# A gradient along rows: the first store held back behind a matmul, and the last but one tile computed and stored in two rows

## The chip, the cores and the metric

The kernel runs on one core of a Trainium2 chip. The metric is the device time of one execution in microseconds (us); the profile's span, which covers the program's own instructions, is 1.8 to 2.6 us shorter.

## The reference, cut to what matters

```python
def setup_inputs():
    return {"x": np.random.randn(8192, 8192).astype(np.float32)}

def reference(x):
    return np.gradient(x, axis=1)
```

Inside a row the result is half the difference of the two neighbours; at both ends it is the plain difference. 268 MB are read and 268 MB written, and there is almost no arithmetic.

## The kernel before

The matrix is cut into 32 tiles of 128 partitions by two rows of 8192 floats (8.39 MB). Three slots hold them. A tile is loaded to column 64 of its slot, the vector engine writes half the differences from column 0, and the store reads from there. All loads and stores are issued by one engine (SyncE) into one queue, in the order three loads, three stores, three loads, and so on.

```python
    with tc.manual_schedule():
        for i in range(NB):                      # NB = 3
            load(i)
        for i in range(nsets):                   # nsets = 32
            ...
            ins = nc.gpsimd.tensor_sub(out=ends[:, i, :, :], ...)   # both edges, waits for the load
            at = [chain(i, ins, loads[i])]
            last = i == nsets - 1
            nr = 1 if last else R                # R = 2 rows; the last tile goes row by row
            for r in range(0, R, nr):
                ...
                ins = nc.vector._custom_dve(dve_ops.TENSOR_TENSOR_REDUCE_SUB_MAX, out=b[:, c0:c1],
                    in0=b[:, SH + c0 + 1 : SH + c1 + 1], in1=b[:, SH + c0 - 1 : SH + c1 - 1], ...)
                halved = chain(i, ins, *at)
                placer = nc.gpsimd if i % 5 in (1, 3) and not last else nc.vector
                ins = placer.tensor_copy(out=res[:, :, 0 : m : m - 1], in_=ends[:, i, r : r + nr, :])
                placed = chain(i, ins, halved)
                ins = nc.sync.dma_start(out=out_sets[i, :, ...], in_=b[:, ...])
                stores[i] = chain(i, ins, placed)
                at = [halved]
            if i % NB == NB - 1:
                for k in range(i + 1, min(i + 1 + NB, nsets)):
                    load(k)                      # waits for the store of the same slot
```

The edge copy (`tensor_copy`) puts the two end columns into the result; of every five tiles two have it done by GpSimd, the others by the vector engine.

## Time and profile before

| | before |
|---|---|
| median at first, 3 runs | 1247.24 us (1247.1 to 1248.14) |
| span of the profiled run | 1245.0 us |
| vector engine busy | 45% |
| DMA, mean over the span | 431 GB/s |

The DMA engines bound the kernel; the prediction shows the lines. A "turn" below is the point where the queue passes from loads to stores or back: near 62, 178, 294 us from loads to stores, near 120 and 236 back to loads. In the windows of the DMA, the share of a 1 us stretch in which exactly sixteen 64 KB packets start (1049 GB/s), one on each engine, is at once their mean duration in us. The usual one is 2.42. In the kernel before, the last packets ahead of the turns near 120, 178 and 236 (the turn near 62, at 3.37, stands in the prediction; columns: stretch, its length, vector engine, GpSimd, clock, DMA share, GB/s):

```profile
116.90:117.90 1.00, 0.00 (x0) 0.00 (x0) 1.00 2.42 1049
174.80:175.80 1.00, 1.00 (x1) 0.00 (x0) 1.00 2.42 1049
232.90:233.90 1.00, 0.00 (x0) 0.00 (x0) 1.00 2.42 1049
```

These three turns cost nothing; of the first four, only the one near 62 did.

### The profile page before, as it was taken

Reading aid. Unit: us, or ns where it says so; the run is one execution under the profiler, and the core shown is the slowest. Engines: PE = TensorE matmul, PEld = TensorE weight load, DVE = VectorE, ACT = ScalarE, POOL = GpSimd, SP = SyncE. Lnnn points to the kernel's source line nnn. Section 1 sums busy time; section 2 is a strip of 40 time slices with the busy share of each in tenths; the row PEclk is TensorE's granted clock in tenths of the full one; section 3 lists DMA queues with packets and bytes.
Section 4 is the critical chain, followed back from the end, with each engine's and each line's share of the span. In section 5 each row is a group of like instructions: output and inputs, shape, how many; then the busy total and the mean of one; then the engine's idle time right before and its main releaser. Section 6 shows DMA issues by size and latency. Waiting matters only on the chain.

```text
span 1245.0 us, 241 instructions
## 1 busy us (share of the span) xinstructions
DVE 554.8 (45%) x54; POOL 8.8 (1%) x48
## 2 busy tenths in 40 slices
DVE  2850483079009603850582079009603840591083
POOL 0000000000000000000000000000000000000000
DMA  9999999999999999999999999999999999999999
GB/s 404 438 436 419 425 438 438 438 438 438 434 427 421 436 438 438 436 438 432 432 419 438 436 438 432 436 434 432 423 436 436 436 438 436 430 427 430 436 411 404
DMA packets 9361, 536.88 MB, mean 431 GB/s; under 512 B 1040, under 2 KB 1040, under 8 KB 1040
## 3 DMA queue, kind: packets, MB, share of 16 engines
q1 hardware_dynamic: 9360, 536.88, 99.8%
q14 instruction: 1, 0.01, 0.0%
HBM read 268.44 MB, written 268.44 MB: 431 GB/s over the span
## 4 chain that ended last, share of the span: by engine, by line
another core or an unknown queue 74%; DVE 18%; DMA 3%; issue 2%; POOL 1%; SPq 0%; POOLq 0%
DVE slot L81 18%; DMA slot<-in_x_dram 3%; POOL ends L70 0%; POOL slot L92 0%; SPq L60 0%; DVE slot L92 0%; POOLq L127 0%
## 5 line engine op out<-in xcount | busy, mean ns | idle before, releaser
L81 DVE CUSTOM_DVE_ANT_0 slot<-slot 128x16382 f32<-128x16382 f32 (+1 forms) x33 | 551.3, 16706 | 667.9 <-POOL ends L70 667.9
L70 POOL TENSOR_TENSOR ends<-slot 128x4 f32<-128x4 f32 x32 | 6.3, 198 | 988.8 <-DMA slot<-in_x_dram 988.8
L92 DVE COPY slot<-ends 128x4 f32<-128x4 f32 (+1 forms) x21 | 3.6, 172 | 0.7
L92 POOL COPY slot<-ends 128x4 f32<-128x4 f32 x12 | 2.3, 190 | 207.9 <-DVE slot L81 207.9
L116 POOL MEMSET const-bfloat16-1.0<- 128x1 bf16 x1 | 0.1, 102 | 0.0
L116 POOL MEMSET const-uint8-127<- 128x1 uint8 x1 | 0.1, 102 | 0.0
L116 POOL MEMSET const-float32-0.0<- 128x1 f32 x1 | 0.1, 99 | 0.2 <-issue 0.2
L116 POOL MEMSET const-float32-1.0<- 128x1 f32 x1 | 0.1, 99 | 0.0
## 6 DMA issues: line engine op xcount, KB each, us to landing
out_dram<-slot SPq DMA_DIRECT2D x2, 4096.0 KB, 20.2
slot<-in_x_dram SPq DMA_DIRECT2D x32, 58.0
out_dram<-slot SPq DMA_DIRECT2D x31, 40.3
```

Source lines behind the costliest of these rows:

```text
L70: ins = nc.gpsimd.tensor_sub(out=ends[:, i, :, :], in0=xin[:, :, 1 : m : m - 2], in1=xin[:, :, 0 : m - 1 : m - 2],)
L81: ins = nc.vector._custom_dve(dve_ops.TENSOR_TENSOR_REDUCE_SUB_MAX, out=b[:, c0:c1], in0=b[:, SH + c0 + 1 : SH + c1 + 1], in1=b[:, SH + c0 ...
L92: ins = placer.tensor_copy(out=res[:, :, 0 : m : m - 1], in_=ends[:, i, r : r + nr, :])
L116: nc = _bacc.Bacc("TRN2", target_bir_lowering=False, num_devices=1)
```

## The change

It has two intents. The first store, which stood in the queue from 40 us on, is to come after the third load is through, so that it finds every engine idle. And tile 30, the last but one, is to be stored in halves so that its first half is in the queue before the last load ends.

```diff
+    psum = ctx.enter_context(tc.tile_pool(name="psum", bufs=1, space=bass.MemoryType.PSUM))
+    unread = psum.tile([1, 128], f32, name="unread", tag="unread")
...
+    def follow(ins, needed, reason):
+        edge = mybir.DependencyInfo(mybir.DependencyClass.Sync, mybir.DependencyReason.DATA)
+        tc.add_manual_dep(ins.ins, needed.ins.name, edge, reason=reason)
...
-            last = i == nsets - 1
+            last = i >= nsets - 2
...
-                placer = nc.gpsimd if i % 5 in (1, 3) and not last else nc.vector
+                placer = nc.gpsimd if i % 5 in (1, 3) and not last or i == nsets - 2 else nc.vector
...
+                if i == 0:
+                    at = [halved]
+                    first = placed
+                    continue
+                if i == 1:
+                    pause = nc.tensor.matmul(
+                        out=unread[:], lhsT=slots[0][:, 0:1], rhs=slots[0][:, 0:128], start=True, stop=True
+                    )
+                    follow(pause, placed, "towards the end of the third load")
+                    follow(store(0, 0, R, first), pause, "after the third load")
+                store(i, r, nr, placed)
```

The matmul's result is never read; it is a delay.

More of the change, by code (lines that the diff above doesn't have):

```diff
@@ L4 @@
 import concourse.tile as tile
-from concourse import bass_utils, dve_ops
+from concourse import bass_utils, dve_ops, mybir
 from concourse._compat import with_exitstack
@@ L61, in load, with store @@
         loads.append(chain(i, ins, *([stores[i - NB]] if i >= NB else [])))
+    def store(i, r, nr, *needed):
+        ins = nc.sync.dma_start(
+            out=out_sets[i, :, r * m : (r + nr) * m], in_=slots[i % NB][:, r * m : (r + nr) * m]
+        )
+        stores[i] = chain(i, ins, *needed)
+        return ins
     with tc.manual_schedule():
@@ L90 @@
                 res = b[:, r * m : (r + nr) * m].rearrange("p (t m) -> p t m", m=m)
-                placer = nc.gpsimd if i % 5 in (1, 3) and not last else nc.vector
+                placer = nc.gpsimd if i % 5 in (1, 3) and not last or i == nsets - 2 else nc.vector
                 ins = placer.tensor_copy(out=res[:, :, 0 : m : m - 1], in_=ends[:, i, r : r + nr, :])
                 placed = chain(i, ins, halved)
-                ins = nc.sync.dma_start(
-                    out=out_sets[i, :, r * m : (r + nr) * m], in_=b[:, r * m : (r + nr) * m]
-                )
-                stores[i] = chain(i, ins, placed)
+                if i == 0:
[5 more added lines that the diff above has]
+                        out=unread[:], lhsT=slots[0][:, 0:1], rhs=slots[0][:, 0:128], start=True, stop=True
+                    )
+                    follow(pause, placed, "towards the end of the third load")
+                    follow(store(0, 0, R, first), pause, "after the third load")
+                store(i, r, nr, placed)
                 at = [halved]
```

## The prediction

> **What bounds the kernel now.** I read the page first, then the waits, then the order in time at both ends, then the DMA windows in 1 us steps. The page (busy time of the engines, then the DMA part):
>
> ```profile
> span 1245.0 us, 241 instructions
> ...
> DVE 554.8 (45%) x54; POOL 8.8 (1%) x48
> ...
> DMA  9999999999999999999999999999999999999999
> ...
> HBM read 268.44 MB, written 268.44 MB: 431 GB/s over the span
> ```
>
> No compute engine is busy for half of the span and the 16 DMA engines are full in every slice, so the kernel ends when 536.88 MB have passed through them. The unit is one load or store of 8.39 MB. In order of time, GpSimd's first small operation on a tile starts when that tile's load has landed, so its start times are landing times. Here are the first two groups of three loads (first column start in us, second duration):
>
> ```profile
> 22.70 0.20 POOL L70 TENSOR_TENSOR ends<-slot 128x4 f32<-128x4 f32 x1 [22.26 <-DMA slot<-in_x_dram]
> ...
> 42.04 0.20 POOL L70 TENSOR_TENSOR ends<-slot 128x4 f32<-128x4 f32 x1 [19.14 <-DMA slot<-in_x_dram]
> ...
> 59.56 0.19 POOL L92 COPY slot<-ends 128x4 f32<-128x4 f32 x1 [17.32 <-DVE slot L81]
> 62.45 0.20 POOL L70 TENSOR_TENSOR ends<-slot 128x4 f32<-128x4 f32 x1 [2.71 <-DMA slot<-in_x_dram]
> ...
> 139.84 0.20 POOL L70 TENSOR_TENSOR ends<-slot 128x4 f32<-128x4 f32 x1 [77.19 <-DMA slot<-in_x_dram]
> ...
> 159.18 0.20 POOL L70 TENSOR_TENSOR ends<-slot 128x4 f32<-128x4 f32 x1 [1.64 <-DMA slot<-in_x_dram]
> ...
> 178.54 0.20 POOL L70 TENSOR_TENSOR ends<-slot 128x4 f32<-128x4 f32 x1 [19.16 <-DMA slot<-in_x_dram]
> ```
>
> From the second to the third landing takes 20.41 us in the first group and 19.36 in the second; first to second is 19.34 in both. Six transfers lie between the landings at 139.84 and 255.87 (the next group), 116.03 us, so one transfer takes **19.34 us** (434 GB/s). 64 of them are 1237.7 us. The other 7.3 us of the span are: the first landing 3.4 us later than one transfer, 1.07 us in the third load, 0.9 us of closing steps after the last store (whose wait ends at 1244.14), and about 2.0 us in the later groups: the landings at 62.45 and 1205.53 are 59 transfers apart, 1143.08 us against 1141.06. The later third loads took 19.36, 19.36, 19.39, 19.85, 19.96, 20.01, 19.52, 19.62 and 19.35, so the loss sits at the turn from loads to stores, and not in every group.
>
> The DMA windows (last column GB/s, by when a packet starts; 1049 is sixteen packets of 64 KB, one per engine) show both places that the change touches:
>
> ```profile
> 58.00:59.00 1.00, 1.00 (x1) 0.00 (x0) 1.00 3.37 1049
> 59.00:60.00 1.00, 0.49 (x1) 0.19 (x1) 1.00 0.00 0
> 60.00:61.00 1.00, 0.00 (x0) 0.00 (x0) 1.00 0.00 0
> 61.00:62.00 1.00, 0.00 (x0) 0.00 (x0) 1.00 2.28 983
> ```
>
> ```profile
> 1202.00:1203.00 1.00, 1.00 (x1) 0.00 (x0) 1.00 0.61 262
> 1203.00:1204.00 1.00, 0.81 (x2) 0.00 (x0) 1.00 0.00 0
> 1204.00:1205.00 1.00, 0.00 (x0) 0.00 (x0) 1.00 2.30 983
> 1205.00:1206.00 1.00, 0.24 (x1) 0.20 (x1) 1.00 0.15 66
> ```
>
> The third load's last sixteen packets start in 58 to 59 us and the first store's in 61 to 62: the share 3.37 says that these took 3.37 us each where 2.42 is usual. At the tail only four packets start in 1202 to 1203, none in the next us, and all sixteen engines start again after 1204: twelve engines stood idle for 1 to 2 us, because the store of tile 30 was issued at 1203.88, when four late engines were just finishing their last load.
>
> **What the Trainium skill says.** "DMA: Bandwidth & Descriptors", Where 436 GB/s comes from, gives a ceiling of 435 GB/s; the trace's 434 agrees, so nothing is to be had from the rate. The same page, Queues, rings and completion order, says that each engine consumes descriptors in ring order; the trace agrees, as the store issued at 40.39 moves nothing until the third load is through, over 20 us later. Its Latency and other measured facts puts the first byte of such an issue at about 0.6 us; here it is longer: the issue at 1203.88 starts packets after 1204.5 (in half-us windows, 1966 GB/s in 1204.5 to 1205.0), some 0.9 us, and the first load at 0.74 starts packets in 1.5 to 2.0. "TensorE: Matmul & The Clock Gate", Single matmul latency, gives (219 + N)/1.2 ns for a lone cold bf16 matmul, 0.29 us at N = 128; this one is float32, for which I estimate 0.3 to 0.9 us. The kernel before has no matmul, so no trace here shows it.
>
> **The change part by part.**
> *First store.* It is no longer issued at 40.39 but after a matmul that waits for tile 1's edge copy (59.56 + 0.19 = 59.75). With 0.6 us for the matmul the issue comes at about 60.4 to 60.7, and the first packets 0.9 us on, at **61.3 to 61.6**. The third load has no store behind it. I take its last packets to need the usual 2.42 us, ending at 60.6 to 61.2, with a landing at 42.04 + 19.34 = 61.4 instead of 62.45. So the 1.07 us of slow packets are exchanged for 0.3 to 1.0 us of idle engines: the first store starts 0 to 0.5 us earlier than before, I take **0.3**. The second store is issued directly behind it, far ahead of its turn, so no later wait moves.
> *Later turns.* All engines begin the first store together. In the tail of the kernel before, an idle start put 15 of 16 first packets in the same half us. If the 2.0 us of later loss come of engines that have drifted apart (four were about 2 us late at the end), a common start might shrink it; the trace does not show the cause, and the second group lost nothing without any such start. I count half: **1.0 us**, the least certain term.
> *Tile 30 in two rows.* One vector instruction of 17.23 us becomes two of about 8.69 (tile 31 already runs so), and GpSimd's two copies of 0.19 lie beside them. The first half's store is issued near 1186.42 + 8.7 + 0.3 = 1195.4, some 8 us before the ring runs dry, so the idle stretch of the twelve engines goes. But the end is set by the four late engines, which had none: from the last landing (1205.53) to the end of the last store's wait is 38.61 us, two transfers at 19.34 being 38.68. The tail loses nothing on the path, so this part is worth **0** while the same engines are late, up to a few tenths otherwise. The vector engine is free at 1203.8, before tile 31 lands; its two halves and stores stay hidden behind the store of tile 30.
> Sum: 0.3 + 1.0 + 0 = 1.3 us off a span of 1245.0. The median of 1247.24 is 2.2 above the span, and I keep that: 1247.24 - 1.3 = 1245.9.
>
> **The rivals.** (a) The matmul, the only one of the program, on an engine that has done nothing for 60 us, takes 1.5 to 3 us with its waits, and the idle gap outgrows the slow packets: 1248 to 1250. For it: no row to read its cost from. Against it: a semaphore releases GpSimd's copy within 0.1 us in this trace. (b) The load-to-store loss comes of the turn from reading to writing, not of drift, and engines in step all pay it at once, 1 us at each of ten turns as in the first group: some 1255. Against it: the engines were within half a us of each other at the second turn, which cost nothing. (c) All drift goes: 2.0 + 0.3 off, 1244.9. (d) The tail's gap is worth its full 2 us: against it stand the 38.61 us.
>
> **Range and chances.** Removing all loss after the start (1.07 + 2.0 us) without any idle gap ends at 1244.2, the low edge. The high edge is the slow matmul of (a) at its milder end with no gain elsewhere, 1248.0; the three runs before also spread over 1.0 us. For 2% the time would have to move by 25 us, far more than any rival gives: within 2% at 0.98.
>
> **What would show it.** A matmul of under 1 us from about 59.8, and the store's issue after it near 60.6; in the windows, last load packets of the usual length, then an empty us, then sixteen packets together near 61.5; the third landing near 61.4. The later third-load distances tell whether the drift shrank: all at 19.34 to 19.4 is rival (c), all at 20.4 is (b). At the tail a store issue near 1195, no empty us, and again 38.6 us from the last landing to the end. The prediction is wrong if the first store's packets start after 62, or if the late turns lose much more than 2 us.

## The result, and the profile after

| | before | after |
|---|---|---|
| median, 4 runs each | 1247.42 us (1247.1 to 1248.14) | 1249.51 us (1248.56 to 1249.63) |
| ratio | | 1.0014, 95% interval 0.9997 to 1.0032 |
| span of the profiled run | 1245.0 us | 1247.1 us |

A ratio is the mean time of one kernel's fast runs over that of the other's fast runs of the same rounds, so it is not quite the ratio of the medians. The class "within 2%" was right. The time was not: 1245.9 was predicted, and 1249.51 lies above the range's high end of 1248.0. By these runs alone the interval still just reaches 1.0; every kernel with the late store in the experiments lay on the same side.

In order of time (start, duration), the profile after shows the matmul, the issue behind it, the early landings and the end:

```profile
41.91 0.20 POOL L84 TENSOR_TENSOR ends<-slot 128x4 f32<-128x4 f32 x1 [19.12 <-DMA slot<-in_x_dram]
...
59.67 0.59 PE L116 MATMUL unread<-slot 128*1 128x128 f32 x2 [59.67 <-POOL slot L106]
60.29 18.98 SPq L71 DMA_DIRECT2D out_dram<-slot  x3
61.25 0.20 POOL L84 TENSOR_TENSOR ends<-slot 128x4 f32<-128x4 f32 x1 [1.63 <-DMA slot<-in_x_dram]
...
140.23 0.20 POOL L84 TENSOR_TENSOR ends<-slot 128x4 f32<-128x4 f32 x1 [78.78 <-DMA slot<-in_x_dram]
...
159.58 0.20 POOL L84 TENSOR_TENSOR ends<-slot 128x4 f32<-128x4 f32 x1 [1.64 <-DMA slot<-in_x_dram]
...
179.93 0.20 POOL L84 TENSOR_TENSOR ends<-slot 128x4 f32<-128x4 f32 x1 [20.15 <-DMA slot<-in_x_dram]
...
1188.33 17.42 DVE L95 CUSTOM_DVE_ANT_0 slot<-slot 128x8190 f32<-128x8190 f32 x2 [59.85 <-POOL ends L84]
1197.08 8.91 POOL L106 COPY slot<-ends 128x2 f32<-128x2 f32 x2 [8.79 <-DVE slot L95]
1205.82 19.88 SPq L71 DMA_DIRECT2D out_dram<-slot  x4
```

The third load lands 19.34 us after the second (61.25 less 41.91), where it was 20.41 before: its slow packets are gone. But the landing at 179.93 comes 20.35 us after the one at 159.58, where it was 19.36: the loss has come back one group later. And at the end GpSimd's two copies take 8.91 us, of which the second takes its usual 0.19, so that the first store of tile 30 goes out at 1205.82 and not near 1195.

The DMA windows of the kernel after (here with columns for TensorE and its weight loads ahead of the vector engine): last packets before the turns near 61, 120, 178 and 236, then the stretch around the first store.

```profile
57.80:58.80 1.00, 0.00 (x0) 0.00 (x0) 1.00 (x1) 0.00 (x0) 1.00 2.42 1049
116.80:117.80 1.00, 0.00 (x0) 0.00 (x0) 0.00 (x0) 0.00 (x0) 1.00 3.18 1049
175.30:176.30 1.00, 0.00 (x0) 0.00 (x0) 1.00 (x1) 0.00 (x0) 1.00 3.43 1049
234.30:235.30 1.00, 0.00 (x0) 0.00 (x0) 0.00 (x0) 0.00 (x0) 1.00 2.42 1049
...
60.00:61.00 1.00, 0.26 (x2) 0.00 (x0) 0.00 (x0) 0.00 (x0) 1.00 0.01 0
61.00:62.00 1.00, 0.00 (x0) 0.00 (x0) 0.51 (x1) 0.20 (x1) 1.00 2.47 1049
```

Near 61 the packets are now of the usual length (2.42). In exchange the turn near 120, free before, costs 3.18 - 2.42 = 0.76 us, and the turn near 178, free before, costs 1.01. The turn near 236 is free again.

Landings, and the issue of the fourth load, which waits for the first store to land, tell where the time went:

| event | before | after | after less before |
|---|---|---|---|
| third load lands | 62.45 | 61.25 | -1.20 |
| first store landed, fourth load issued | 81.78 | 81.14 | -0.64 |
| fourth load lands (turn near 120 passed) | 139.84 | 140.23 | +0.39 |
| seventh load lands (turn near 178 passed) | 255.87 | 257.20 | +1.33 |
| tile 30 lands | 1186.19 | 1188.09 | +1.90 |
| span | 1245.0 | 1247.1 | +2.1 |

### The profile page after: what moved, and what is told of

It reads as the page before. It is cut to its first block, busy times and chain, and to the rows that moved or that the text cites. A ratio compares the mean times of both kernels' runs of the same rounds, so it can differ in the third digit from the quotient of the medians.

```text
span 1247.1 us, 250 instructions
## 1 busy us (share of the span) xinstructions
PE 0.6 (0%) x2; PEld 0.1 (0%) x2; DVE 554.8 (44%) x54; POOL 17.8 (1%) x50
## 4 chain that ended last, share of the span: by engine, by line
another core or an unknown queue 74%; DVE 19%; DMA 3%; POOL 1%; issue 0%; SPq 0%; POOLq 0%
DVE slot L95 19%; DMA slot<-in_x_dram 3%; POOL slot L106 1%; POOL ends L84 0%; SPq L67 0%; DVE slot L106 0%; POOLq L151 0%
## 5 line engine op out<-in xcount | busy, mean ns | idle before, releaser
L106 POOL COPY slot<-ends 128x4 f32<-128x4 f32 (+1 forms) x14 | 11.2, 800 | 216.7 <-DVE slot L95 216.6
```

## The experiments

Twelve kernels ran. Of one call, all ran on the same chip beside runs of the kernel before.

### The parts one by one

Four of the twelve (`rows_only_gpsimd`, `rows_only_vector`, `late_third_store`, `late_fourth_load`) are made from the kernel before, and `before_again` is that kernel. `both_vector` is made from the change, and the other six from the change with tile 30 whole as before.

Theories: the 2 us come of the two turns (turn theory), or of GpSimd's slow copy at the end (copy theory). `late_store_only` is the change with tile 30 whole as before:

```diff
-            last = i >= nsets - 2
+            last = i == nsets - 1
-   placer = nc.gpsimd if i % 5 in (1, 3) and not last or i == nsets - 2 else nc.vector
+   placer = nc.gpsimd if i % 5 in (1, 3) and not last else nc.vector
```

> The late first store alone, tile 30 whole as before. Turn theory (the 2 us come from slow last packets at the turns between loads and stores, which the common start moves and enlarges): 1249.3, the full loss of the change, with the turns near 120 and 178 us each costing 0.7 to 1.0 us. Copy theory (the 2 us come from GpSimd's edge copies of tile 30, which took 8.7 us beside the vector engine): 1247.0, no slower than before.

`rows_only_gpsimd` is the kernel before with the two changed lines of tile 30 (`last`, `placer`) as in the change:

> Tile 30 in two rows with GpSimd's copies alone, the first store early as before. Turn theory: 1247.4, as before, since the stores of tile 30 go out only when GpSimd gets through, within 0.2 us of the whole tile's. Copy theory: 1249.3.

`rows_only_vector` is the kernel before with `last = i >= nsets - 2` alone, so that the vector engine places tile 30's edges:

> Tile 30 in two rows with the vector engine's copies of 0.17 us alone. The first half's store is issued near 1195.5 and the twelve early engines lose no time. If the late engines set the end: 1247.4, within 0.3 of before. If the tail gap was worth its 2 us: 1245.4. If the queued store now makes the last load's last packets slow: up to 1248.4.

`both_vector` is the change with the `placer` line of the kernel before:

> The whole change with tile 30's edge copies on the vector engine instead of GpSimd. Turn theory: 1249.4, as the change. Copy theory: 1247.2 or less.

Measured, five runs each, beside nine runs of the kernel before with a median of 1247.79:

| kernel | median us | ratio (95%) | last packets near 62 / 120 / 178, us |
|---|---|---|---|
| late_store_only | 1249.38 | 1.0011 (0.9998 to 1.0023) | 2.42 / 3.10 / 3.47 |
| both_vector | 1249.34 | 1.0011 (0.9998 to 1.0023) | 2.42 / 3.13 / 3.46 |
| rows_only_gpsimd | 1248.20 | 1.0002 (0.9988 to 1.0015) | 3.53 / 2.42 / 2.92 |
| rows_only_vector | 1248.30 | 1.0001 (0.9989 to 1.0014) | 3.54 / 2.42 / 2.54 |

The two kernels with the late store are some 1.4 us slower by the ratio (each interval just reaches 1.0), the two without it are level with before within the noise, whoever places tile 30's edges. The copy theory falls. In the traces the pattern of the turns is the late store's own: near 120 it costs 0.7 with a late store and nothing without. The runs also answer the tail. In `both_vector` the vector engine's copies let the first half's store out at 1197.09 (start, duration; two stores merged in the second line):

```profile
1188.17 8.69 DVE L95 CUSTOM_DVE_ANT_0 slot<-slot 128x8190 f32<-128x8190 f32 x1 [59.84 <-POOL ends L84]
1196.89 0.17 DVE L106 COPY slot<-ends 128x2 f32<-128x2 f32 x1
...
1197.09 28.46 SPq L71 DMA_DIRECT2D out_dram<-slot  x4
```

That store is over 8 us earlier than in the change, and the median is the same, 1249.34 against 1249.38 with tile 30 whole: filling the tail's idle stretch on the early engines is worth nothing.

### Why the turns: engines in step, or a restart?

The first theory of the turns was the one that the prediction named as a rival: after an idle moment all engines start together, and engines in step (the sixteen last packets near 117 started within 0.14 us of each other after, 0.48 before) pay at a turn. Four kernels test it. `store_after_copy` drops the matmul, so that the first store reaches the engines just as they run dry, one by one:

```diff
-                    pause = nc.tensor.matmul(...)
-                    follow(pause, placed, "towards the end of the third load")
-                    follow(store(0, 0, R, first), pause, "after the third load")
+                    follow(store(0, 0, R, first), placed, "with the second store")
```

> The first store waits for tile 1's edge copy (issue near 59.7) and not for a matmul behind it; tile 30 whole. Its packets should reach the engines near 60.5 to 60.6, just as they finish the third load one by one between 60.3 and 60.8, so that they neither idle much nor start together. In-step theory (a turn costs about 0.7 us when all engines reach it within 0.2 us of each other): the turn near 119 costs nothing if they stay over 0.4 us apart, 0.7 if they fall together. Postponed-turn theory (the first turn from loads to stores with a store already queued costs 1 us, whichever it is): the turn near 177 costs 1.0. Both cheap: 1246.7; turn near 177 dear: 1247.7; both dear: 1248.5.

`late_third_store` leaves the first store early and delays the third:

```diff
+                if i == 2:
+                    follow(store(i, r, nr, placed), stores[1], "after the second store has landed")
```

> The first store is issued early as before; instead the third store waits until the second has landed, near 101, so that the engines idle for about 1.4 us and then start it together. In-step theory: the turn near 62 costs 1.0 as before, and the turn from stores to loads near 121, now in step, costs 0.7, where the kernel before has 0. If the loss at that turn in the change came of something else (the third load's missing queue), it costs 0. The next turn, near 180: 1.0 if it follows from an in-step turn, 0 to 0.5 if the dear one is only ever the first turn from loads to stores. Time: 1248.8 if nothing follows, 1250.5 with both turns dear.

`late_fourth_store` moves the matmul and the held-back store to tiles 4 and 3 (`if i == 3`, `if i == 4`, `store(3, 0, R, first)`):

> The first store early as before, the fourth one late, behind a matmul, so that the engines go idle near 178 instead of near 61. In-step theory: turn near 62 costs 1.0, near 178 nothing but 0.7 us of idle engines, near 237 (stores to loads) 0.7 where before it has 0, and near 295 up to 1.0 where before it has 0.1. If dear turns belong to the start of the program, those near 237 and 295 cost 0 to 0.2. Time: about 1249 against 1247.7.

`dephased` is `late_store_only` with a small extra write, meant to set eight engines apart:

```diff
+                if i == 1:
+                    nc.sync.dma_start(out=out_sets[nsets - 1, 0:8, 0:3072], in_=aside[:, :])
```

> The late first store alone, and between the second and the third store a small write of 12 KB from each of 8 partitions, which gives eight of the engines about 0.45 us more to do and so sets the engines apart after the common start (it writes zeros where the last store writes later). In-step theory: the turn near 120 falls from 0.7 to under 0.2. Otherwise it stays at 0.7. Time: 1249.0 against 1249.4 of the late store alone, within noise; the trace decides.

Measured beside nine runs of before with a median of 1247.59:

| kernel | median us, runs | ratio (95%) | last packets near 62 / 120 / 178 / 236 / 294, us |
|---|---|---|---|
| store_after_copy | 1249.52, 5 | 1.0012 (0.9999 to 1.0026) | 2.42 / 3.04 / 3.37 / 2.42 / 2.46 |
| late_third_store | 1250.92, 4 | 1.0029 (1.0015 to 1.0043) | 3.54 / 3.13 / 3.36 / 2.42 / 3.15 |
| late_fourth_store | 1250.30, 4 | 1.0021 (1.0007 to 1.0035) | 3.40 / 2.42 / 2.42 / 3.10 / 3.55 |
| dephased | 1250.93, 4 | 1.0026 (1.0013 to 1.0040) | see below |

The times of `late_fourth_store` and `dephased` are 1.3 and 1.9 us above what was expected of them, that of `store_after_copy` 1.0 above its dearest case; `late_third_store` is within 0.5 us of its own.

In `late_fourth_store` the idle moment lies near 178, and the dear turns move with it, to the next two (windows: near 62, 178, 236, 294):

```profile
57.80:58.80 1.00, 0.00 (x0) 0.00 (x0) 1.00 (x1) 0.00 (x0) 1.00 3.40 1049
174.80:175.80 1.00, 0.00 (x0) 0.00 (x0) 1.00 (x1) 0.00 (x0) 1.00 2.42 1049
233.80:234.80 1.00, 0.00 (x0) 0.00 (x0) 0.00 (x0) 0.00 (x0) 1.00 3.10 1049
292.30:293.30 1.00, 0.00 (x0) 0.00 (x0) 1.00 (x1) 0.00 (x0) 1.00 3.55 1049
```

In `late_third_store` too the dear turns are the two that follow its idle moment near 101. So it is nothing of the program's start, and not bound to the first store. But the in-step theory does not hold at the turn near 178. There the engines are no longer in step: the sixteen last packets started between 175.52 and 175.98 in the change and between 175.09 and 175.59 in the kernel before, alike, and they cost 1.01 us in the one and 0.01 in the other. In `store_after_copy` they are further apart still, and yet dear (near 117 first, then a stretch of 1 us and one of 2 us near 176):

```profile
116.30:117.30 1.00, 0.00 (x0) 0.00 (x0) 1.00 3.04 1049
175.10:176.10 1.00, 1.00 (x1) 0.00 (x0) 1.00 3.11 983
175.00:177.00 2.00, 2.00 (x1) 0.00 (x0) 1.00 1.68 524
```

The second line holds only fifteen packets; in the third all sixteen start within 2 us, so that the mean is 1.68 x 2 = 3.36 us. This kernel also shows that the length of the idle time matters little. From the end of the third load to the end of the first store it took 19.57 us in the median engine, where 19.32 is usual, so the engines stood idle for about 0.25 us, and both turns were dear all the same. As a test of the turn near 120 it failed: fourteen of its engines began the first store within 0.13 us, so they were nearly in step after all.

`dephased` does not save the theory. The small write took 1.6 to 2.2 us and not 0.45, so eight engines reached the turn about 2 us after the other eight. Those that had no extra write were still in step among themselves (last packets from 117.01 to 117.12) and paid 0.78 us on average. The last packets of the eight that were set apart (118.65 to 119.12) paid only 0.11: six of them nothing, two 0.44. But behind the turn, where the first loads of the change took 2.46 on average, loads are slow here. Sixteen of them, eight of each half, start between 121 and 123 (first line), and their mean is 1.38 x 2 = 2.76 us:

```profile
121.00:123.00 2.00, 0.00 (x0) 0.00 (x0) 0.00 (x0) 0.00 (x0) 1.00 1.38 524
175.90:177.90 2.00, 0.00 (x0) 0.00 (x0) 2.00 (x1) 0.00 (x0) 1.00 1.58 524
```

The fourth load lands 81.69 us after the third, 2.67 more than the 79.02 of `late_store_only`, of which the small write explains 2.2 at most. Setting engines apart moved the cost of this turn and did not lower it; that being in step is part of its cause is not shown. At the turn near 178 (second line) sixteen packets spread over 1.7 us still lasted 1.58 x 2 = 3.16 us.

For the whole a second theory was formed, the restart theory: once the engines have run dry, loads pay some 0.7 us more where they are first met, and the first turn from loads to stores costs 1.0 again. (The first store packets after a restart pay almost nothing: 2.47 in the change.) The numbers suggested it: the very first load packets of every kernel take 0.6 to 0.8 us longer than 2.42, and the first turn to stores then costs 1.0; after a restart with stores, the first turn to loads costs 0.7 and the first turn to stores 1.0. It predicts what a restart with loads does, and that the length of the pause does not matter to the turns. `late_fourth_load`:

```diff
         loads.append(chain(i, ins, *([stores[i - NB]] if i >= NB else [])))
+        if i == 3:
+            follow(ins, stores[2], "after the third store has landed")
```

> Stores as before, but the fourth load waits until the third store has landed, near 120.7, so that the engines go idle for 1.7 to 2 us and start again with loads. Restart theory (after the engines have run dry, the first packets of loads are slow by 0.7 us wherever loads are first met, and the next turn from loads to stores costs 1.0 again; everything after is cheap): first packets of the fourth load 0.7 slow as those of the program's first load, turn near 180 (loads to stores) 1.0 where before it has 0 to 0.5, turn near 239 (stores to loads) 0. In-step theory: the engines start together, so the turn near 180 costs 1.0 and the one near 239 0 to 0.7. Start-with-stores theory (only a restart that begins with stores is dear): turn near 180 costs 0 to 0.5. Time by the restart theory: 1250.8 against 1247.6.

`longer_pause` puts the matmul in `for _ in range(8)`:

> The late first store behind eight matmuls instead of one, tile 30 whole: issue near 62.9 instead of 60.3, so the engines are idle for 3.3 us instead of 0.7. Restart theory: the two turns cost the same 0.7 and 1.0, only the idle time grows, 1252.0. If the dear turns came of the short gap itself (the store reaching the engines while the last load packets are still being finished), they fall to 0 and it is 1250.3.

`two_late_stores` has `if i in (0, 3)`, `if i in (1, 4)` and `store(i - 1, 0, R, first)`:

> The first and the fourth store both late, each behind a matmul, tile 30 whole. Restart theory: turn near 119 0.7, idle 0.7 near 179, turn near 238 0.7 again, turn near 297 1.0; 1250.8. If a kernel pays for a restart only once: turns near 238 and 297 cost 0 to 0.4, 1249.3.

`before_again` is the kernel before, unchanged:

> The kernel before, unchanged, as a second look at its turns and at the noise: ratio to itself within 0.1%. Turn near 62 1.0, turn near 119 0, turn near 178 0 to 0.5.

Measured beside seven runs of before with a median of 1248.10:

| kernel | median us, 4 runs | ratio (95%) | last packets near 62 / 120 / 178 / 236 / 294, us |
|---|---|---|---|
| late_fourth_load | 1251.79 | 1.0032 (1.0017 to 1.0047) | 3.55 / 2.42 / 3.39 / 2.42 / 2.62 |
| longer_pause | 1252.38 | 1.0036 (1.0021 to 1.0051) | 2.42 / 3.15 / 3.50 / 2.42 / 2.56 |
| two_late_stores | 1250.44 | 1.0023 (1.0007 to 1.0040) | 2.42 / 3.13 / 2.42 / 3.12 / 3.47 |
| before_again | 1247.66 | 0.9999 (0.9984 to 1.0014) | 3.42 / 2.42 / 2.57 / 2.42 / 2.52 |

`late_fourth_load` in windows: near 62, the restart itself, near 178 and near 236:

```profile
57.80:58.80 1.00, 1.00 (x1) 0.00 (x0) 1.00 3.55 1049
...
121.50:122.50 1.00, 0.00 (x0) 0.00 (x0) 1.00 2.85 983
177.80:178.80 1.00, 1.00 (x1) 0.00 (x0) 1.00 3.39 1049
236.80:237.80 1.00, 0.00 (x0) 0.00 (x0) 1.00 2.42 1049
```

The second line holds fifteen packets (983), so one took 2.85 x 16 / 15 = 3.04 us: the first load packets after the restart are 0.62 slow, like those of the program's first load. The turn to stores near 178 costs 0.97, and the next turn to loads nothing. All three are what the restart theory said, and the start-with-stores theory falls. Near 178 the sixteen packets started over 0.64 us, no closer than in the kernel before, which again speaks against the in-step theory at the turn to stores. In `longer_pause` an idle time some 3 us longer (the store's issue moved from 60.5 in `late_store_only` to 63.45) leaves both turns at 0.73 and 1.08; in `two_late_stores` each of two restarts makes the next turn to loads dear (0.71 and 0.70), and the turn to stores after the second costs 1.05. The times follow within 1 us: 1250.8, 1252.0 and 1250.8 were expected. `before_again` shows the noise, 0.9999, and that the turn near 178 costs 0.15 in a second trace.

The packets of all fourteen traces say how sharp this is: but for the first turn to loads after a restart with stores, no turn to loads costs anything (2.42 to 2.43), and no turn to stores but the first after a restart costs more than 0.73.

No experiment pointed to a kernel faster than the one before: apart from the idle stretch at its tail, which was worth nothing, it has one restart alone, the one at its start.

## Why the prediction was wrong

**The bound** was right: the DMA engines set the end in every kernel here.

**First store, 0.3 us gained:** right, and somewhat under. The matmul is two passes that end after 0.59 us (0.6 was taken), the issue came at 60.29 (60.4 to 60.7), the third landing at 61.25 (61.4), and the store's packets began in 61 to 62. The first store had landed 0.64 us earlier than before, of which 0.13 was there at the second landing already (41.91 against 42.04).

**Later turns, 1.0 us gained:** this step failed, by its sign. The prediction took a common start for something that can only help the drift of the engines. The runs show that what comes with it, engines that have run dry, is paid for afterwards: 0.76 us at the next turn to loads and 1.01 at the next turn to stores, both free before. The 1.07 us that the early store cost near 62 was not removed, it was postponed to 178. The net is -0.64 at the first store, +1.33 at the seventh landing. Rival (b) was named with 1 us at each of ten turns; it happened at two, and at the dearer of them the engines were not in step. The prediction's own sign of being wrong came true: from the third landing to the last it took 1146.17 us, 5.1 more than 59 transfers, where it was 2.0 before (some 0.6 of it the idle stretch behind the third load). Rival (a) did not happen; that the measured time lies in its 1248 to 1250 is chance. Rival (c) did not happen either, and (d), the tail's gap, was worth nothing in `both_vector`.

**After the seventh landing** nothing systematic is left. From there to tile 30's landing it took 930.3 and 931.3 us in the two traces of the kernel before, 930.7 and 931.0 in the two with tile 30 in rows alone, and 930.9, 931.5 and 930.5 in the three with the late store of the change. The further 0.57 us between the two profiled runs of before and after are within that spread.

**Tile 30, worth 0:** the size was right, the working wrong. The prediction laid GpSimd's copies of 0.19 us beside the vector engine's second row. The first of them took 8.91 - 0.19 = 8.72 us, about as long as the 8.69 of that row. The Trainium skill says why one should expect it: "SBUF — State Buffer", Who interferes with whom, says that a vector instruction with two SBUF inputs contends with a GpSimd instruction that reads SBUF, that the port which they share is an exclusive lock, and that the order of issue decides which one waits. The vector operation here has two SBUF inputs, the copy reads SBUF and began just behind it; the 8.72 us agree. In the kernel before, these copies ran with the vector engine idle, so their 0.19 us was no measure of this. It cost nothing because of the step that held: the late engines set the end. From the last landing to the end of the last packets it took 38.2 us before and 38.3 after.

**What stays open** is what goes on inside a DMA engine that makes the first turn after a restart dear; whether the engines being in step has a part in the 0.7 us at the turn to loads, which no run separated from the restart; and why the later turns to stores cost the kernel before anything from 0 to 0.4 us (up to 0.7 in others, far from any restart). The runs show when the cost appears, not its cause.

## What to carry to other kernels

Where one DMA queue bounds a kernel, do not let it run dry to tidy up a slow spot: a restart cost its idle time, and here some 1.7 us more at the next two turns, wherever it was tried (for a restart with loads, on its first packets and at the next turn to stores). When a wait or a slow packet disappears at one place, follow the landings for two more groups before counting it as gained. And take the duration of a GpSimd instruction only from a row in which its neighbours on the vector engine were as busy as they will be.

## What the Trainium skill lacked or had wrong

- "DMA: Bandwidth & Descriptors" has nothing on the cost of a turn between loads and stores in one queue, or on its coming back after the engines have run dry: 0.6 to 0.8 us at the first turn to loads, or on the first load packets, and 0.9 to 1.1 at the first turn to stores, on the last packets before it, in the traces here with a restart (in `dephased` the cost is spread over more packets); 0 to 0.7 at the other turns to stores, and nothing at the other turns to loads.
- The same page's first-byte latency of about 0.6 us for an issue from SyncE does not say from where it is counted. In the kernel before, packets began some 0.9 us after the start of the issue at 1203.88; the issuing instruction itself takes 0.34 us (the median of the loads), so that from its end the figure would be near the page's.
- "TensorE: Matmul & The Clock Gate" gives the latency of a lone bf16 matmul only; the float32 one here, with 128 columns, ran as two passes of 0.37 and 0.42 us that overlap, 0.59 us in all.
- "DMA: Bandwidth & Descriptors" has no figure for a small write between two large stores: 12 KB on each of eight engines took 1.6 to 2.2 us, where the bytes alone would have taken an estimated 0.45 us at the rate of the large packets (64 KB in 2.42 us).
